# The first stage of a hybrid layer kernel in another order: conditioning and token norms among the filters, float32 filters, loads on three queues

## The chip, the cores and the metric

The kernel runs on one core of a Trainium2 chip. A core has five engines with an instruction stream each: TensorE (PE, matmuls and transposes), VectorE (DVE), ScalarE (ACT), GpSimd (POOL) and SyncE (SP), which here only issues transfers. Sixteen DMA engines move data between HBM and the on-chip memory SBUF; matmuls write to PSUM, which has eight banks. The engines meet through semaphores. The metric is the device time of one execution in microseconds (us); a kernel's time is the median of its runs.

## The reference, cut to what matters

The layer takes 1024 latent tokens, 256 context tokens and two conditioning vectors, in float32. What the change touches stands first:

```python
ada_x = jnp.split(silu(c) @ w_ada[l] + b_ada[l], 6, axis=-1)      # w_ada: 1024 x 6144
ada_c = jnp.split(silu(c_ctx)[None] @ w_ada[l] + b_ada[l], 6, axis=-1)
hc = modulate(rmsnorm(ctx, norm_mix_g[l]), ada_c[0], ada_c[1])    # 256 tokens
hx = modulate(rmsnorm(x, norm_mix_g[l]), ada_x[0], ada_x[1])      # 1024 tokens
h = jnp.sin(z @ w1 + b1); h = jnp.sin(h @ w2 + b2)                # hyena_filters
h = (h @ w3).reshape(L, 2, 2, 512) * jnp.exp(-t * deltas)[:, None, None, :]
Kf = jnp.fft.rfft(k, n=2 * L, axis=0)                             # k: the two sides of h
...
yx, _ = token_mixer(hx, ...)      # w_in projections, Hyena, chunkwise mLSTM, merge
x = x + ada_x[2][:, None, :] * yx
aff = jax.nn.softmax(hx2 @ w_router); gate, idx = lax.top_k(jnp.swapaxes(aff, 1, 2), 128)
ye = (silu(xg @ w1) * (xg @ w3)) @ w2 * gate      # 16 experts, 128 tokens each
return rmsnorm(x + ada_x[5][:, None, :] * scattered_ye, final_norm_g)
```

## The kernel before

Float32 products are made of three matmuls in a rounded format (float32r): each operand is split into a high part (a cast on ACT) and a low part (a subtraction), and `mm3` multiplies high by high, high by low and low by high. A plain float32 matmul needs no split; the profile shows it as two records.

**The first stage** runs to about 165 us. It makes the spectrum of the Hyena filters and the modulated, transposed tokens that the projections multiply.

- `filter_mlp` makes the filter network's hidden rows (`fh`, split into `hl`) and the split last-layer weights (`whh`, `wll`, from the sums `w3sd` that POOL makes). `skip_row` is one small float32 matmul for each order.
- The filters are made in eight units (kind, order, half of the channels). `filter_taps(u)` has 16 matmuls, eight with `whh` on 128 weight rows and eight with `wll` on 64, and four DVE operations that multiply by the decay table `dec` into `fs` (through `fsf`). `filter_dft(u)` multiplies the taps by the DFT table `ft` into four PSUM banks `fe`; `filter_out(u)` combines these on DVE and POOL (`fk_t`, `fk`) and stores them to `K_d`.
- `unit(u)` is `filter_dft(u)`, then `filter_taps(u+2)`, then `filter_out(u)`. Other generators are stepped in between: with `run((a, 1), (some(b, 2), 1))` a step of one stands in the program behind a step of the other.
- `ada_group(0)` is the conditioning: eight slabs `wada` of 1 MB, four matmuls for each into `ada`, four transposes `adaT`. Four slab buffers exist, so slab 4 is loaded when slab 0 has been multiplied. `columns` transposes the small vectors loaded as `R`.
- `norm_tokens` squares and sums token tiles on ACT, makes the reciprocal root (`rq_v`, `rq_r`) on DVE and scales the tiles (`xl`, `xt`) on DVE. `modulated_T` has eight steps for a group of tiles: transposes on PE, scale and shift on ACT or DVE (`hxf`), a split. `gc` makes the context tokens (`hc`), `g0` and `g1` the two halves of the latent tokens (`hx`). The projections that follow start with the matmuls into `pj`, whose weights are `whi` and `wlo`.

All PSUM tiles come from one pool of eight banks; `w2` is a pool of 12 small SBUF tiles. After the filter network the recording layer lets the engines' streams be reordered; the tables of rows further down show the result.

**Later.** The projections and mixers follow, then the router: DVE finds the 128 best tokens of each expert by 16 rounds of MAX8, FIND_INDEX8 and MATCH_REPLACE8. Meanwhile `fill` loads the first expert slabs `er` and splits them into `eh` (ACT) and `el`; with `PAIR` = 4 split slabs made before the experts start, the subtraction of slab 2 is POOL's and those of slabs 0, 1 and 3 are DVE's. The chosen tokens are gathered (`xg`), transposed and modulated by `gather_T` (`xgf`, split into `xgh` and `xgl`), and the experts' matmuls (`pup`, `acc`) start. At the end the final norm takes `rsqrt` of two tiles at a time; POOL multiplies some tiles by the gain `tg`.

Of the kernel before, what the change touches and what calls it, by code (L numbers as in the profile page):

```python
# [103 lines left out]
def layer_kernel(ctx: ExitStack, tc: tile.TileContext, A: dict, out: bass.AP, dbg=None, stop=None):  # L104
# [23 lines left out]
    def w2(shape, dt=F32, name="w"):  # L128
        return wk.tile(shape, dt, name=name, tag="w2", bufs=12)
# [104 lines left out]
    def ada_group(g, wtile, ahead=2):  # L234
# [53 lines left out]
    def filter_loads(alA, alB, alC):  # L288
        zt = alB([33, 1024], name="zt", tag="ss0", bufs=4)
# [11 lines left out]
        R3 = w2([16, 128], name="R3")  # L301
        SY.dma_start(R3[0:8], rows("c", 0, 8))
        SY.dma_start(R3[8:16], rows("c_ctx", 0, 8))
        small.update(R3=R3)
# [9 lines left out]
        def last_layer(o):  # L314
            sd = alB([128, 2, 512], name="w3sd", tag=f"ss{o}", bufs=4)
# [11 lines left out]
    def filter_mlp(alA, alB, loads, tables):  # L327
# [3 lines left out]
        h1 = alB([128, 512], name="fh1", tag="ss0", bufs=4)  # L331
# [10 lines left out]
        for _ in range(4):  # L342
            next(tables)
# [11 lines left out]
        for _ in tables:  # L355
            pass

# [10 lines left out]
        conditions()  # L368

    def filter_tables(al, raw_tile, eng):  # L370
        th, tl = (al([128, len(FT), 128], F32R, name=f"ft{v}") for v in "hl")
        filt["tab"] = th, tl
        raws = []
        for j in range(6):
            raws.append(raw_tile(j))
            SY.dma_start(raws[j], A["ft"][:, 3 * j:3 * j + 3].rearrange("p a m -> p (a m)"))
        yield
        for j in range(6):
            hi, lo = (t[:, 3 * j:3 * j + 3].rearrange("p a m -> p (a m)") for t in (th, tl))
            S.copy(hi, raws[j])  # L380
            eng[j].tensor_tensor(lo, raws[j], hi.bitcast(F32), op=OP.subtract)
            yield

    def filter_taps(u, al):

        kind, o, hf = u
        sets = [[al([128, 4, 256], F32R, name="fs", tag=f"ss{units.index(u) % 2}", bufs=4) for _ in range(2)] for _ in range(2)]
        filt["taps", u] = sets
        hl, whh, wll = filt["hl"], filt["whh"], filt["wll"]
        cs = slice(hf * 256, (hf + 1) * 256)  # L390
        for j2 in range(4):
            p = ps()
            h_ = slice(64 * (j2 // 2), 64 * (j2 // 2) + 64)
            for j in range(2):
                jt = j2 * 2 + j
                pj = p[:, j * 256:(j + 1) * 256]
                T.matmul(pj, hl[:, jt * 128:(jt + 1) * 128], whh[:, o, kind, cs], start=True, stop=False)
                T.matmul(pj, hl[h_, jt * 128:(jt + 1) * 128], wll[h_, o, kind, cs], start=False, stop=True)
            f = w2([128, 2, 256], name="fsf")
            js = slice((j2 % 2) * 2, (j2 % 2) * 2 + 2)  # L400
# [16 lines left out]
    def filter_dft(u):  # L417
# [4 lines left out]
        sets, tabs = filt["taps", u], filt["tab"]  # L422
# [14 lines left out]
    def filter_out(u):  # L437
# [22 lines left out]
        for F, E, a, b, op, rs, rev in ((0, V, bc, bo, OP.add, slice(0, 3, 2), 1), (0, G, bc, bo, OP.subtract, slice(1, 4, 2), 1),  # L460
# [7 lines left out]
            else:  # L468
                res = alC([128, 2, 256], name="fk", bufs=6)
# [43 lines left out]
    alC = phase(sfC, "fC", side="right")  # L513
# [3 lines left out]
    xr = [alxl([128, 1024], name="xr", tag="xl", bufs=4) for _ in range(3)]  # L517
# [1469 lines left out]
```

## Time and profile before

| | before |
|---|---|
| median of 3 runs | 2297.56 us (2296.01 to 2298.42) |
| the profiled execution | 2295.03 us, span 2293.3 us |
| mean granted clock of TensorE | 0.971 |
| PE busy | 2172.0 us (95%), 10609 records |
| DVE busy | 1687.1 us (74%) |
| ACT busy | 1246.8 us (54%) |
| POOL busy | 443.5 us (19%) |
| chain that ended last | PE 48%, DVE 1% of the span, the rest too short or not followed |

The span runs from the first to the last instruction of the profile; the execution's own time is 1.7 us longer. "Busy" counts an engine's instructions and not its waits. The matmul clock has two levels; the profile gives it as a share of the full one. A share of busy time is an average over stages with different limits, so the stage that a change touches has to be looked at by itself.

### The profile page before, as it was taken

To read this page: it belongs to the slowest core of one execution; us is meant where nothing else is said; L and a number is where in the kernel's file an instruction comes from. 1 tells how busy PE (TensorE), PEld (TensorE's weight loads), DVE (VectorE), ACT (ScalarE), POOL (GpSimd) and SP (SyncE) were. 2 spreads that over 40 slices of the span, in tenths; PEclk is the share of its full clock that TensorE was granted. 3 is DMA by queue.
4 is the path that set the end of the run, shared out by engine and by line. 5 is a ranking of instruction groups with operands and counts; after the bars stand their busy time and mean duration, and the time that the engine had idled before them with its cause. 6 is when DMAs were issued, how large, how long until landed. Compare 5 with 4: busy or idle time off the path is not lost. (4 is left out here: it accounts for less than half of the span.)

```text
span 2293.3 us, 28327 instructions
## 1 busy us (share of the span) xinstructions
PE 2172.0 (95%) x10609; PEld 1772.4 (77%) x10609; DVE 1687.1 (74%) x1863; ACT 1246.8 (54%) x1398; POOL 443.5 (19%) x382
## 2 busy tenths in 40 slices
PE   6999999999999999999379999999999999999996
PEld 3679887787778788887268888888888888888884
DVE  5784445664446768553869889898888898888897
ACT  2441342324542223222257777777877777777774
POOL 3563101111124544042200111100111100011001
PEclk9879999999999999999689999999999999999998
DMA  7243335555563333864769999999999999999993
GB/s 264 93 139 95 113 114 176 176 195 190 177 199 114 110 115 124 300 223 147 271 216 386 380 386 382 378 379 393 381 385 384 379 377 396 380 386 383 380 349 141
DMA packets 234793, 605.18 MB, mean 264 GB/s; under 512 B 17722, under 2 KB 89462, under 8 KB 231456
## 3 DMA queue, kind: packets, MB, share of 16 engines
q1 hardware_dynamic: 216752, 551.44, 65.7%
q0 software_dynamic: 12128, 41.43, 5.7%
q10 hardware_dynamic: 5776, 10.50, 1.2%
q8 instruction: 83, 1.36, 0.2%
q14 instruction: 54, 0.44, 0.1%
HBM read 539.34 MB, written 63.98 MB: 263 GB/s over the span
## 5 line engine op out<-in xcount | busy, mean ns | idle before, releaser
L98 DVE TENSOR_TENSOR el<-er,eh 128x2048 fp32r<-128x2048 f32 x383 | 874.4, 2290 | 115.4 <-ACT eh L98 102.5
L98 ACT CAST eh<-er 128x2048 fp32r<-128x2048 f32 x384 | 733.7, 1915 | 236.6 <-PE pup L98 169.1
L98 PE MATMUL pup<-eh,xgh 128*128 128x512 f32 x1024 | 319.7, 393 | 1.6 <-ACT xgh L98 1.6
L98 PE MATMUL pup<-eh,xgl 128*128 128x512 f32 x1024 | 316.7, 390 | 0.0
L98 PE MATMUL ps<-hx,whi 128*128 128x512 f32 x960 | 305.4, 399 | 0.0
L98 PE MATMUL pup<-el,xgh 128*128 128x512 f32 x1024 | 274.4, 390 | 0.0
L98 PEld LDWEIGHTS pup<-eh,xgl 128*128 128x128 f32 x1024 | 192.7, 188 | 40.9 <-DVE xgl L98 0.2
L98 PEld LDWEIGHTS pup<-el,xgh 128*128 128x128 f32 x1024 | 192.6, 188 | 40.4
L98 PEld LDWEIGHTS pup<-eh,xgh 128*128 128x128 f32 x1024 | 190.3, 188 | 40.4 <-ACT xgh L98 2.0
L98 PEld LDWEIGHTS ps<-hx,whi 128*128 128x128 f32 x960 | 178.8, 189 | 40.3 <-ACT nt L98 0.8
L98 POOL DMA_INDIRECT acc_d<-ye,idxc x15 | 50.8, 3390 | 747.5 <-DVE ye L98 747.5
L98 PE MATMUL ps<-hx,wlo 128*128 128x512 f32 x480 | 189.9, 396 | 0.0
L98 PE MATMUL acc<-eh,gh 128*128 128x512 f32 x512 | 161.6, 397 | 0.2 <-ACT gh L98 0.2
L98 PE MATMUL acc<-eh,gl 128*128 128x512 f32 x512 | 160.2, 394 | 0.0
L98 PE MATMUL acc<-el,gh 128*128 128x512 f32 x512 | 139.5, 394 | 0.0
L98 PEld LDWEIGHTS acc<-eh,gl 128*128 128x128 f32 x512 | 96.0, 188 | 22.9 <-DVE gl L98 0.4
L98 PEld LDWEIGHTS acc<-el,gh 128*128 128x128 f32 x512 | 96.2, 188 | 22.4
L98 PEld LDWEIGHTS acc<-eh,gh 128*128 128x128 f32 x512 | 95.0, 188 | 21.6 <-ACT gh L98 0.5
L98 PEld LDWEIGHTS ps<-hx,wlo 128*128 128x128 f32 x480 | 90.5, 188 | 21.2
L98 PE MATMUL pg<-hx,gwh 128*128 128x512 f32 x320 | 103.2, 405 | 3.7 <-ACT gwh L98 3.7
L98 ACT ACTIVATE pb<-ps,colv 128x512 f32<-128x512 f32 (+1 forms) x44 | 29.3, 665 | 129.9 <-PE ps L98 122.2
L98 POOL DMA_INDIRECT xg<-xn_d,idxc x16 | 44.9, 2806 | 260.2 <-PE ps L98 226.1
(374 smaller groups left out, 3393.2 us busy)
## 6 DMA issues: line engine op xcount, KB each, us to landing
er<-in_w_exp_dram SPq DMA_DIRECT2D x384, 1024.0 KB, 7.6
wada<-in_w_ada_dram SPq DMA_DIRECT2D x24, 1024.0 KB, 5.0
wraw<-in_w_in_dram SPq DMA_DIRECT2D x30, 512.0 KB, 4.3
K_d<-fk SPq DMA_DIRECT2D x32, 256.0 KB, 2.2
Kt<-K_d SPq DMA_DIRECT2D x16, 512.0 KB, 5.7
v1c<-v_d SPq DMA_DIRECT2D x20, 256.0 KB, 8.0
gwr<-in_w_in_dram SPq DMA_DIRECT2D x20, 256.0 KB, 6.3
eo_d<-eost POOLq DMA_DIRECT2D x16, 256.0 KB, 7.0
```

Source lines behind the costliest of these rows:

```text
L98: r = op(*a, **k)
```

## The change

- The loads of `c` and `c_ctx` go first on SP. The first four `wada` slabs and the token tiles 0 to 7 are issued by POOL, the DFT tables by ACT.
- The order becomes: token loads, conditioning vectors, filter network, `columns`, all eight steps of `ada_group(0)`, the second `last_layer` and `skip_row`, then taps 0 and 1 and the units. The norms and `gc`, `g0` are stepped from unit 0 on; two steps of `g1` stand in the last `filter_dft`.
- `ft` and `fs` stay in float32: no split of either, and `filter_dft` has 16 float32 matmuls for each unit in place of 48 in float32r.
- `filter_taps` takes four PSUM banks at once and runs its eight `whh` matmuls, then its eight `wll` ones.
- `fill` gives POOL the subtractions of the first four slabs. `gather_T` of the first expert has its second half scaled on DVE in place of ACT.
- The final norm's two steps with constants (`v*inv+eps`, `1.5-0.5*v`) are done by ACT.

```diff
-            SY.dma_start(t, w_ada[len(ts) * 128:(len(ts) + 1) * 128, g * 2048:(g + 1) * 2048])
+            (G if g == 0 and len(ts) < ahead else SY).dma_start(t, w_ada[len(ts) * 128:(len(ts) + 1) * 128, g * 2048:(g + 1) * 2048])
...
+    def filter_tables(al):
+        ft = al([128, len(FT), 128], name="ft")
+        filt["tab"] = ft
         for j in range(6):
+            S.dma_start(ft[:, 3 * j:3 * j + 3], A["ft"][:, 3 * j:3 * j + 3])
...
+        for high in (True, False):
+            for jt in range(8):
+                tap(jt, high)
         for j2 in range(4):
...
-            hi, lo = sets[j2 // 2]
-            S.copy(hi[:, js], f)
-            (V if u == units[0] else G).tensor_tensor(lo[:, js], f, hi[:, js].bitcast(F32), op=OP.subtract)
...
-                    mm3(p[:, h * 256:(h + 1) * 256], [x[:, i] for x in tabs], [x[:, k % 4] for x in sets[k // 4]],
-                        j == 0, j == 1)
+                    T.matmul(p[:, h * 256:(h + 1) * 256], tab[:, i], sets[k // 4][:, k % 4], start=j == 0, stop=j == 1)
...
-            SY.dma_start(toks[i], src)
+            (G if i < 8 else SY).dma_start(toks[i], src)
...
+    load_tokens(0, 1, 2, 3, 4, 5, 6, 7)
+    load_small()
+    conditions()
+    filter_mlp(alA, alB, fl)
     in_order[0] = False
+    columns()
+    for _ in ag0:
+        pass
     filt["last_layer"](1)
     filt["skip_row"](1)
-    load_tokens(0, 1, 2, 3)
-    run((filter_taps(units[1], alB), 1), (some(ag0, 1), 1))
+    run((filter_taps(units[0], alB), 1))
+    run((filter_taps(units[1], alB), 1))
...
+    unit(0, (nt, 1))
+    run((nt, 1))
+    unit(1, (some(gc, 4), 1), (nt1, 1))
+    unit(2, (gc, 1))
...
+    unit(3, (some(g0, 4), 1), (nt1, 1))
+    unit(4, (some(g0, 2), 1), (nt, 1))
+    unit(5, (some(g0, 1), 1))
...
+    unit(6, (g0, 1))
+    run((filter_dft(units[7]), 1), (some(g1, 2), 1))
...
-            (G if i == 2 else V).tensor_tensor(lo, raws[i], hi.bitcast(F32), op=OP.subtract)
+            (G if i < PAIR else V).tensor_tensor(lo, raws[i], hi.bitcast(F32), op=OP.subtract)
...
+                    if on[n]:
+                        S.activation(f[:, k], src, AF.Identity, scale=sc, bias=sh)
+                    else:
+                        V.tensor_scalar(f[:, k], src, sc, sh, op0=OP.mult, op1=OP.add)
...
+        S.activation(v, ss, AF.Identity, scale=inv, bias=cs2[:, 0:1])
...
+        S.activation(v, v, AF.Identity, scale=-0.5, bias=cs2[:, 1:2])
```

On PE, at the start of the program, these rows stood before (`sil` is the activated conditioning vector, `fh` and `fw` the filter network, `whh` and `wll` the taps' weights):

```order
L98 MATMUL ps<-zt,fw_116 64x512 x2
L98 MATMUL ps<-fh_161,fw_120 64x512 x2
L98 MATMUL ps<-fw_127,fh_162 1x512
L98 MATMUL ps<-cst,sil 128x16
L98 MATMUL ps<-whh,hl 128x256
L98 MATMUL ps<-wll,hl 128x256
L98 MATMUL ps<-whh,hl 128x256
L98 MATMUL ps<-wll,hl 128x256
```

Now the same place reads as follows, up to the first DFT:

```order
L98 MATMUL ps<-cst,sil 128x16
L98 MATMUL ps<-zt,fw_119 64x512 x2
L98 MATMUL ps<-fh_187,fw_123 64x512 x2
L98 MATMUL ps<-fw_127,fh_188 1x512
L98 MATMUL ps<-cst,R_171 128x128
L98 MATMUL ps<-cst,R_176 128x44
L98 MATMUL ada<-wada,s_pad 32x512 x32
L98 MATMUL adaT<-cst,ada_sb 128x128 x4
L98 MATMUL ps<-fw_128,fh_188 1x512
L98 MATMUL ps<-whh,hl 128x256 x8
L98 MATMUL ps<-wll,hl 128x256 x8
```

All 32 `ada` matmuls now stand ahead of the first taps, where they used to be spread over units 0 to 3 and the taps of unit 1, and the taps' matmuls stand in two blocks of eight.

On POOL, behind its first small settings, these rows stood before (`w3sd` and `wll` belong to the filters' last layer, `ftl` is the low part of the tables, `fs` the low part of the taps):

```order
L98 MEMSET afp 128x192
L98 ISA
L98 TENSOR_TENSOR w3sd<-fw_127 128x512 x2
L98 TENSOR_TENSOR wll<-w3sd,whh 128x1024
L98 TENSOR_TENSOR ftl<-xr,fth 128x384 x4
L98 TENSOR_TENSOR w3sd<-fw_128 128x512 x2
```

Now POOL's stream begins with twelve transfers; the brackets name the semaphores that a row waits for, and DMASW0 to DMASW3 rise when slabs 0 to 3 have landed:

```order
L98 DMA wada<-in_w_ada_dram 128x2048 x4
L98 DMA xl<-in_ctx_dram 128x1024 x2
L98 DMA xt<-in_x_dram 128x1024 x2
L98 DMA xt<-in_x_dram 128x1024 [waits DMASW0_49]
L98 DMA xt<-in_x_dram 128x1024 [waits DMASW1_49]
L98 DMA xl<-in_x_dram 128x1024 [waits DMASW2_49]
L98 DMA xl<-in_x_dram 128x1024 [waits DMASW3_49]
L98 MEMSET afp 128x192
L98 ISA
L98 TENSOR_TENSOR w3sd<-fw_127 128x512 [waits DMAHW7_49,DMAHW6_49]
```

POOL's first `w3sd` therefore stands behind the landing of the first four slabs.

On DVE, in the router's search for the best tokens, this is the fifth and sixth round before:

```order
L98 MAX vals<-aw 48x8
L98 TENSOR_TENSOR el<-er,eh 128x2048
L98 MATCH_REPLACE aw<-vals,aw 48x512
L98 MAX_INDEX idxu<-vals,aw 48x8
L98 MAX vals<-aw 48x8
L98 TENSOR_TENSOR el<-er,eh 128x2048
L98 MATCH_REPLACE aw<-vals,aw 48x512
L98 MAX_INDEX idxu<-vals,aw 48x8
```

Now the rounds follow one another, and POOL has the four subtractions ahead of its gather of the tokens:

```order
L98 DMA grow_9220<-in_b_ada_dram 128x1024
L98 TENSOR_TENSOR el<-er,eh 128x2048 x4
L98 DMA xg<-xn_d,idxc 128x1024
```

Three `el` rows have left DVE's stream between the router's result and the end of the search; POOL's one became four.

## Rows read from the trace of the kernel before

**Rows 1.** The page's second part: busy tenths of PE in 40 slices of 57 us.

```profile
PE   6999999999999999999379999999999999999996
```

**Rows 2.** Busy time by stretch, with granted clock, DMA share and GB/s.

```profile
core 0: us, PE busy (x) PEld busy (x) DVE busy (x) ACT busy (x) POOL busy (x), PEclk, DMA share, GB/s
...
24.00:165.00 141.00, 132.51 (x643) 94.87 (x643) 98.08 (x170) 57.10 (x102) 67.36 (x52) 0.86 0.43 155
...
60.00:150.00 90.00, 85.83 (x438) 64.81 (x438) 67.31 (x119) 40.20 (x75) 50.98 (x42) 0.80 0.28 94
...
1165.00:2240.00 1075.00, 1075.00 (x4888) 887.25 (x4887) 960.51 (x563) 839.15 (x655) 95.00 (x30) 1.00 1.00 378
```

**Rows 3.** PE's timeline, 24 to 49 us: start, duration, then operation.

```profile
24.70 0.58 PE L98 MATMUL ps<-whh,hl 128*128 128x256 f32 x1
...
32.86 1.86 PE L98 MATMUL ps<-fw,fh 64*1 64x512 f32 x2
...
36.69 1.93 PE L98 MATMUL ada<-wada,s_pad 128*32 128x512 f32 x8
...
48.34 1.05 PE L98 MATMUL ada<-wada,s_pad 128*32 128x512 f32 x2
```

**Rows 4.** Transfers from 0 to 60 us: GB/s in 40 slices of 1.5 us.

```profile
GB/s 0 118 54 6 276 235 216 330 373 240 352 336 385 202 1 257 415 410 431 437 426 421 401 407 410 180 93 382 224 0 0 0 104 377 418 412 407 369 22 0
```

**Rows 5.** PE's timeline: a DFT's end and the taps behind it.

```profile
98.14 0.40 PE L98 MATMUL fe<-fs,fth 128*128 128x256 f32 x2
...
98.50 0.40 PE L98 MATMUL fe<-fs,fth 128*128 128x256 f32 x2
...
99.51 0.38 PE L98 MATMUL ps<-wll,hl 64*128 64x256 f32 x1
99.82 0.39 PE L98 MATMUL ps<-whh,hl 128*128 128x256 f32 x1
...
103.04 0.58 PE L98 MATMUL ps<-whh,hl 128*128 128x256 f32 x1
```

**Rows 6.** PE's timeline, 162 to 179 us: the projections' start and `g1`'s transposes.

```profile
162.41 0.39 PE L98 MATMUL pj<-whi,hch 128*128 128x264 f32 x1 [2.83 <-ACT whi L98]
...
164.99 0.59 PE L98 MATMUL pj<-wlo,hch 128*128 128x264 f32 x1 [0.41 <-DVE wlo L98]
...
177.56 0.39 PE L98 MATMUL pj<-whi,hx 128*128 128x264 f32 x1 [1.08 <-DVE hx L98]
177.78 1.03 PE L98 MATMUL ps<-cst,xl 128*128 128x128 f32 x8
```

**Rows 7.** DVE's timeline in the router's search, 1119 to 1127 us.

```profile
1119.70 0.67 DVE L98 MAX8 vals<-aw 48x8 f32<-48x512 f32 x1
...
1121.75 0.67 DVE L98 MAX8 vals<-aw 48x8 f32<-48x512 f32 x1
1122.34 2.26 DVE L98 TENSOR_TENSOR el<-er,eh 128x2048 fp32r<-128x2048 f32 x1
...
1125.86 0.67 DVE L98 MAX8 vals<-aw 48x8 f32<-48x512 f32 x1
```

**Rows 8.** POOL's timeline beside that search.

```profile
1116.65 4.52 POOL L98 TENSOR_TENSOR el<-er,eh 128x2048 fp32r<-128x2048 f32 x1 [0.89 <-ACT eh L98]
1155.33 1.03 POOL L98 DMA_INDIRECT xg<-xn_d,idxc  x1 [34.17 <-DVE idxl L98]
```

**Rows 9.** The experts' start: PE's first matmul, ACT's work ahead of it.

```profile
1163.46 1.22 PE L98 MATMUL pup<-eh,xgh 128*128 128x512 f32 x2 [1.65 <-ACT xgh L98]
...
1161.04 1.86 ACT L98 ACTIVATE xgf<-ps,AB 128x128 f32<-128x128 f32 x5 [42.68 <-issue]
```

**Rows 10.** The tail's timelines: DVE's constant steps and POOL's product.

```profile
2270.97 0.16 DVE L98 TENSOR_SCALAR rq_v<-rq_v 128x2 f32<-128x2 f32 x1
...
2278.12 2.26 DVE L98 TENSOR_SCALAR rq_v<-rq_v 128x2 f32<-128x2 f32 x1
...
2278.02 2.34 POOL L98 TENSOR_TENSOR xf<-xf,tg 128x1024 f32<-128x1024 f32 x1 [1.54 <-ACT xf L98]
```

More of the change, by code (lines that the diff above doesn't have):

```diff
@@ L288, in filter_loads @@
     def filter_loads(alA, alB, alC):
-        zt = alB([33, 1024], name="zt", tag="ss0", bufs=4)
+        R3 = w2([16, 128], name="R3")
+        SY.dma_start(R3[0:8], rows("c", 0, 8))
+        SY.dma_start(R3[8:16], rows("c_ctx", 0, 8))
+        small.update(R3=R3)
+        zt = alB([33, 1024], name="zt", tag="ss0", bufs=3)
         SY.dma_start(zt, A["zT"])
@@ L325, in filter_loads, with filter_mlp @@
         return zt, w1, bb, w2_, w3
-    def filter_mlp(alA, alB, loads, tables):
+    def filter_mlp(alA, alB, loads):
         zt, w1, bb, w2_, w3 = loads
-        h1 = alB([128, 512], name="fh1", tag="ss0", bufs=4)
+        h1 = alB([128, 512], name="fh1", tag="ss0", bufs=3)
         h2 = alB([128, 512], name="fh2", tag="ss1", bufs=4)
@@ L341, in filter_mlp @@
         p = ps()
-        for _ in range(4):
-            next(tables)
         for n in range(2):
@@ L367, in filter_mlp @@
         skip_row(0)
[L368 to L373, printed above, removed]
-        for j in range(6):
[L375 to L382, printed above, removed]
+    def filter_tables(al):
+        ft = al([128, len(FT), 128], name="ft")
+        filt["tab"] = ft
+        for j in range(6):
+            S.dma_start(ft[:, 3 * j:3 * j + 3], A["ft"][:, 3 * j:3 * j + 3])
     def filter_taps(u, al):
         kind, o, hf = u
-        sets = [[al([128, 4, 256], F32R, name="fs", tag=f"ss{units.index(u) % 2}", bufs=4) for _ in range(2)] for _ in range(2)]
+        sets = [al([128, 4, 256], name="fs", tag=f"ss{units.index(u) % 2}", bufs=3 + units.index(u) % 2) for _ in range(2)]
         filt["taps", u] = sets
@@ L390, in filter_taps, with tap @@
         cs = slice(hf * 256, (hf + 1) * 256)
-        for j2 in range(4):
[L392 to L400, printed above, removed]
+        pt = [ps() for _ in range(4)]
+        def tap(jt, high):
+            pj = pt[jt // 2][:, (jt % 2) * 256:(jt % 2 + 1) * 256]
+            h_ = slice(0, 128) if high else slice(64 * (jt // 4), 64 * (jt // 4) + 64)
+            T.matmul(pj, hl[h_, jt * 128:(jt + 1) * 128], (whh if high else wll)[h_, o, kind, cs], start=high and jt % 2 == 0, stop=not high and jt % 2 == 1)
+        for high in (True, False):
+            for jt in range(8):
+                tap(jt, high)
+        for j2 in range(4):
+            p = pt[j2]
+            f = sets[j2 // 2][:, (j2 % 2) * 2:(j2 % 2) * 2 + 2]
             V.scalar_tensor_tensor(f, p.rearrange("p (j c) -> p j c", j=2), -1.0 if kind and j2 > 1 else 1.0,
@@ L516, in layer_kernel @@
     fl = filter_loads(alA, alB, alC)
-    xr = [alxl([128, 1024], name="xr", tag="xl", bufs=4) for _ in range(3)]
-    ft0 = filter_tables(alB, lambda j: xr[j // 2][:, (j % 2) * 512:(j % 2) * 512 + 384], [G, G, G, G, V, V])
-    next(ft0)
+    filter_tables(alB)
     dec = alA([128, 8, 512], name="dec")
@@ L560, in unit @@
         run((filter_out(units[u]), 1), *more)
-    unit(0, (some(ag0, 1), 1))
-    columns()
-    load_tokens(4, 5, 6, 7)
-    nt = norm_tokens(0, 1, 2, 3)
-    unit(1, (some(ag0, 2), 1), (some(nt, 2), 1))
-    unit(2, (some(ag0, 2), 1), (nt, 1))
-    nt = norm_tokens(4, 5, 6, 7)
-    unit(3, (ag0, 1), (nt, 1))
     sada.close()
-    sfC.close()
     AB = cp.tile([128, 2, 2, 8], F32, name="AB")
@@ L619, in layer_kernel @@
     g1 = hx_gen(1)
-    unit(6, (some(g0, 2), 1))
-    run((filter_dft(units[7]), 1))
+    unit(6, (g0, 1))
+    run((filter_dft(units[7]), 1), (some(g1, 2), 1))
     sfB.close()
@@ L1888, in layer_kernel, with rsqrt_s @@
     warm = late([128, 1], F32, name="warm")
+    cs2 = late([128, 2], F32, name="cs2")
+    V.memset(cs2[:, 0:1], EPS)
+    V.memset(cs2[:, 1:2], 1.5)
+    def rsqrt_s(ss, n, inv):
+        v, r = sm([128, n], name="rq_v"), sm([128, n], name="rq_r")
+        S.activation(r, ss, AF.Sqrt, scale=inv, bias=cs2[:, 0:1])
+        S.activation(v, ss, AF.Identity, scale=inv, bias=cs2[:, 0:1])
+        V.reciprocal(r, r)
+        V.tensor_tensor(v, v, r, op=OP.mult)
+        V.tensor_tensor(v, v, r, op=OP.mult)
+        S.activation(v, v, AF.Identity, scale=-0.5, bias=cs2[:, 1:2])
+        V.tensor_tensor(r, r, v, op=OP.mult)
+        return r
     tg = spare([128, 2, 1024], name="tg")
```

30 lines of the change are left out of this document (10 added, 20 removed).

## The prediction, made before the changed kernel was run

> **What bounds the kernel now.** I read the busy slices first [rows 1]: PE is full nearly everywhere, and the places where it is not are the start, the dip near 1110 to 1165 us and the end. The change edits just these three, so each is costed by the engine that is late there. Between 1165 and 2240 us PE is busy for all of 1075 us [rows 2], so whatever the experts' start gains is still there at the end; I take the same of the mixer stages between. For the first stage I then read the windows: from 24 to 165 us PE is busy for 132.5 of 141 us and DVE for 98.1 [rows 2]. PE is the bound there, and it doesn't run at its full level: the mean granted clock from 60 to 150 us is 0.80 [rows 2]. The stage's end is the first matmul into `pj` at 162.41 and the first with `wlo` at 164.99 [rows 6].
>
> **First stage: PE's own work.** A tap matmul follows the last one after 0.31 us at the full level (99.51 to 99.82), while three DFT matmuls of the same 256 columns take 0.36, or 0.12 each (98.14 to 98.50) [rows 5]. The taps alternate between 128 and 64 weight rows. The extra 0.19 can belong to the change of rows, or the pair's 0.38 to the 64-row matmul itself. In the first case a unit's 16 taps now cost 16 x 0.12 and two changes, 2.3 us, in the second 5.0 as before; over eight units the ends are 22 us apart. A 64-row float32 matmul of 512 columns (`skip_row`) took 1.86 us at the lower level [rows 3], which is 0.93 at the full one; four transposes of 128 columns, float32 too and on 128 rows, took 1.03 there [rows 6]. So 64 rows alone cost nothing extra. I take 2.3. The Trainium skill, TensorEngine Tiling (Array Packing), section Tiling Modes, says that a change of the tiling mode, other than of the tile, drains the engine; by that rule the grouping is worth its 22 us at the full level, and by a price of the 64-row matmul itself it would be worth nothing.
>
> A unit's DFT was 48 matmuls of 0.12, 5.8 us. Now it is 16 in float32. Their price from the same `skip_row`: 1.86 us for 512 columns at the lower level is 0.46 for 256 at the full one; from the transposes, eight records (four transposes of 128 columns) in 1.03 [rows 6], 0.4 to 0.5 for 256. I take 0.43: 6.9 us for a unit, 1.1 more than before. Beside this, `gc` and `g0` with 16 steps and two steps of `g1` are 3.2 + 6.4 + 1.6 us (0.4 for the two transposes of a `gc` step, 0.8 for the four of the others). From the first tap to the first `pj` PE then has 8 x 2.3 + 8 x 6.9 + 11.2 = 84.8 us of work at the full level.
>
> **First stage: the late start.** Taps began at 24.70 [rows 3]. They now stand behind all eight `ada` steps, and these behind the slabs. By the tiles' shapes 16.9 MB move first (eight slabs 8.4, eight token tiles 4.2, `dec` 2.1, tables 1.2, last-layer weights 1.0), and some 0.3 of small loads. The slices move 400 to 437 GB/s when large tiles are queued and 330 to 385 with `dec` and smaller ones [rows 4]. The first 13 MB take 32 us at 410; the last four slabs wait for buffers, so they start when `ada` does, and 4.2 MB take 10 us more. POOL's queue waits for slabs to land ahead of its first `w3sd`, and PE's `skip_row` and `ada` stand behind what follows from it, so `ada` doesn't start before about 32 us either way. An `ada` step is 1.93 us at the lower level and 1.05 at the full one [rows 3]; the slabs, not PE, set the pace. With the last step, the copy, `adaT` and `skip_row` behind the landing at 44 to 47 I put the first tap at 52 us (48 to 60). The Trainium skill, DMA: Bandwidth & Descriptors, section Issuing engines are not separate DMA queues, says that loads started from several engines share the same 16 engines and only save issue time; by that rule three queues bring no bandwidth and the sum of bytes above holds, whereas if a second queue doubled the rate the start would be near 35. The slices at 437 from SP alone [rows 4] agree with the rule.
>
> **First stage: what PE waits for.** DVE loses only the few splits that it had and what moves ahead of the taps, and gains two steps of `g1`: of its 98.1 us I keep 92 (85 to 98). So DVE, not much shorter than before, is now as long as PE's 84.8, and where DVE has all eight PSUM banks (the taps take four at once) PE waits. I add 8 us for the difference and 4 for ends of units and for `whi` (2.83 [rows 6]). PE comes from `ada` steps with gaps, and before the change it was at the lower level there (0.58 per tap, 1.93 per step [rows 3], whatever the clock column says); two units of taps and half a DFT at that level are 8 us more. Sum: 52 + 84.8 + 12 + 8 = 157 for the first `pj`, against 162.41: -6. The two `g1` steps taken out of the projections (0.8 each) and the waits there for `hx` (one of 1.08 [rows 6]; with a first half ready earlier it goes) are -3. First stage: -9, from -24 (first tap at 48, no cold units, 8 us of waits) to +5 (first tap at 60, full low-level units). ACT's casts and POOL's subtractions of `fs` (POOL was busy for 67 of 141 us [rows 2]) I cost at nothing: the taps are made two units ahead of their DFT. If that cover is gone, taking them away gains up to 2 us a unit for units 0 and 1.
>
> **The experts' start.** A round of the search takes 2.05 us (1119.70 to 1121.75) and one with an `el` 4.11 (1121.75 to 1125.86) [rows 7]. Three go: -6.2. POOL's four at 4.52 are 18 us from 1116, so done near 1134, ahead of its gather at 1155 [rows 8]; that idle stretch is the cover, and without it the gather would be later by what sticks out. POOL's subtraction ran beside rounds of unchanged length. ACT had five `xgf` of 0.35 ahead of the first `xgh`, now four; PE's first `pup` waited for `xgh` [rows 9]: -0.3. Sum -6.5 (-4.5 to -7).
>
> **The tail.** A constant step takes 0.16 us on DVE, but 2.26 when POOL's product of 2.34 starts just before [rows 10]; the chain of waits has three of these, 6.3 us too long together. On ACT they aren't held, but ACT has squares and a scaling of 1.1 us each ahead of them. I take half: -3.5 (0 to -6).
>
> **Sum.** -9 - 6.5 - 3.5 = -19 on the profiled execution's 2295.0: 2276. The runs' median lies 2.5 above that execution: 2278.5.
>
> **The rivals.** (a) The clock decides, and the result is slower. Half as many but four times as long matmuls make a low level dear: the DFTs alone then cost 13.8 us a unit. PE's 84.8 us need 106 at the mean of 0.80 that 60 to 150 us had, about what I forecast with its waits; they need 128 at 0.66, the forecast's 105 and 23 more, and then the 19 are gone and about 2302 is reached. Against it: in the trace the level fell while alternating taps ran (0.39 a matmul at 99.82, 0.58 at 103.04 [rows 5]), and these go; float32 matmuls keep PE denser. For it: PE's new waits for DVE. 8 in 100. (b) The start is later than 60: `R` and the last-layer weights stand behind the large tiles in three queues, and the first tap comes at 65. Then the first stage gives +4 and the sum is -6: 2291.5. 14 in 100. (c) The later edits give nothing, since POOL's four subtractions and ACT's chain are late themselves: 2288.5. 10 in 100. (d) PE is dense and at the full level from the first unit: -24 - 6.5 - 4 gives 2263. 16 in 100. My forecast has 52.
>
> **The numbers.** 0.2%, 4.6 us, is about what a measurement of this kernel can tell from no change. Faster by more than that (below 2293) are the forecast, (c), (d) and two thirds of (b): 0.88. (a) is slower in five cases of eight, 0.05; the rest, 0.07, lies within. The range of 2265 to 2291 leaves out (a), some of (b) and the far end of (d). The likeliest's own is 2271 to 2285.
>
> **What would show it.** First tap at 52 and 16 tap matmuls in 2.3 us at the full level; 16 float32 matmuls of 0.43; PE waiting for DVE at the DFTs' starts; first `pj` at 157. Rounds of 2.05 throughout the search and the first `pup` 6.5 us nearer to the search's start. No `rq_v` above 0.3 us at the end. Wrong would be a granted clock below 0.7 between 52 and 157, a first tap past 60, taps still at 5 us a unit, or PE waiting for slabs after 1165.

## The result and the profile after

The changed kernel takes 2279.01 us (median of 4, 2277.28 to 2282.55) against 2297.99 (2296.01 to 2302.77) for the kernel before, measured together with it: a ratio of 0.9921, 95% interval 0.9907 to 0.9934. The prediction was 2278.5, within 2265 to 2291. The time came out as forecast, but not by the steps of the forecast: the start was 11 us later and PE's stretch behind it some 15 us shorter than forecast, a wait for weights was twice its size, and the tail's term gave nothing. That these errors cancel is luck.

The profiled execution took 2278.72 us, its span 2277.0. Four landmarks place the difference to the span of 2293.3 before: the first tap, the first `pj`, the first MAX8 of the search and the experts' first `pup`. The rows of before for them are [rows 3, 6, 9]; the first MAX8 is this row of DVE's timeline, before and after:

```profile
1113.55 0.69 DVE L98 MAX8 vals<-ps 48x8 f32<-48x512 f32 x1 [1.14 <-PE ps L98]
```

```profile
1103.54 0.69 DVE L98 MAX8 vals<-ps 48x8 f32<-48x512 f32 x1 [1.14 <-PE ps L98]
```

| us | before | after | after minus before |
|---|---|---|---|
| first tap | 24.70 | 63.27 | +38.6 |
| first `pj` | 162.41 | 157.90 | -4.5 |
| first MAX8 of the search | 1113.55 | 1103.54 | -10.0 |
| first MAX8 to first `pup` | 49.91 | 43.51 | -6.4 |
| first `pup` to the end | 1129.84 | 1129.95 | +0.1 |

The page's second part after, PE's busy tenths, and the windows (columns as in [rows 2]):

```profile
PE   2989999999999999999289999999999999999996
```

```profile
24.00:63.00 39.00, 17.45 (x78) 2.93 (x74) 11.48 (x17) 5.85 (x9) 10.89 (x8) 0.91 0.70 260
63.00:150.00 87.00, 84.11 (x441) 70.72 (x440) 78.29 (x152) 36.13 (x65) 34.38 (x26) 0.96 0.26 88
60.00:150.00 90.00, 86.40 (x454) 71.22 (x446) 78.86 (x157) 38.02 (x68) 34.38 (x26) 0.96 0.25 85
1147.00:2220.00 1073.00, 1072.95 (x4871) 885.38 (x4872) 957.43 (x563) 836.35 (x653) 94.06 (x29) 1.00 1.00 377
```

PE's first slice fell from 6 to 2 tenths [rows 1]: between 24 and 63 us it works for 17.45 of 39 us, where it had taps before. From then on it is dense, and at 0.96 of its full level between 60 and 150 us where it had 0.80 [rows 2]. The experts are as full as they were.

PE's timeline after, which answers to [rows 3], and its last DFT and first projections, which answer to [rows 6]:

```profile
34.62 1.86 PE L98 MATMUL ps<-fw,fh 64*1 64x512 f32 x2 [9.18 <-ACT fh L98]
41.99 0.45 PE L98 MATMUL ps<-cst,R 128*128 128x128 f32 x1 [5.50 <-DMA R<-in_hy_conv_dram]
...
43.14 5.55 PE L98 MATMUL ada<-wada,s_pad 128*32 128x512 f32 x32
50.25 1.06 PE L98 MATMUL ada<-wada,s_pad 128*32 128x512 f32 x8 [1.56 <-DMA wada<-in_w_ada_dram]
...
59.30 1.73 PE L98 MATMUL ada<-wada,s_pad 128*32 128x512 f32 x8 [0.55 <-DMA wada<-in_w_ada_dram]
...
63.27 1.22 PE L98 MATMUL ps<-whh,hl 128*128 128x256 f32 x8
64.42 0.75 PE L98 MATMUL ps<-wll,hl 64*128 64x256 f32 x8
65.10 1.21 PE L98 MATMUL ps<-whh,hl 128*128 128x256 f32 x8
...
66.92 7.17 PE L98 MATMUL fe<-fs,ft 128*128 128x256 f32 x32
...
145.91 3.62 PE L98 MATMUL fe<-fs,ft 128*128 128x256 f32 x16
157.90 0.59 PE L98 MATMUL pj<-whi,hch 128*128 128x264 f32 x1 [8.37 <-ACT whi L98]
...
159.42 0.57 PE L98 MATMUL pj<-wlo,hch 128*128 128x264 f32 x1
```

Four slabs are multiplied in one go at 43.14: they had long landed (POOL's waits for them end by 23.86), and PE waited for `R`. A unit's 16 taps take 65.10 - 63.27 = 1.83 us, its DFT 6.8 (66.92 to 73.74, where the next tap starts). The last DFT ends at 149.5; then PE stands 8.37 us for `whi`. The queue of SP and ACT's cast show that wait's other end:

```profile
96.52 55.80 SPq L400 DMA_DIRECT2D K_d<-fk  x23
152.43 1.06 SPq L630 DMA_DIRECT2D wraw<-in_w_in_dram  x2
```

```profile
156.78 1.07 ACT L98 CAST whi<-wraw 128x1056 fp32r<-128x1056 f32 x1 [6.47 <-DMA wraw<-in_w_in_dram]
```

The first projection weights stand on SP behind 23 stores of filters, each of which waits for its `fk`; they land 4.3 us after their issue (152.43 to 156.78).

The search and the experts' start after (DVE, POOL and PE; [rows 7 to 9] before):

```profile
1105.62 0.67 DVE L98 MAX8 vals<-aw 48x8 f32<-48x512 f32 x1
...
1107.66 0.67 DVE L98 MAX8 vals<-aw 48x8 f32<-48x512 f32 x1
...
1109.71 0.67 DVE L98 MAX8 vals<-aw 48x8 f32<-48x512 f32 x1
```

```profile
1105.78 17.95 POOL L98 TENSOR_TENSOR el<-er,eh 128x2048 fp32r<-128x2048 f32 x4
1139.12 1.03 POOL L98 DMA_INDIRECT xg<-xn_d,idxc  x1 [15.38 <-issue]
```

```profile
1147.05 1.22 PE L98 MATMUL pup<-eh,xgh 128*128 128x512 f32 x2 [1.49 <-ACT xgh L98]
```

All rounds take 2.04 to 2.08 us, and POOL is done at 1123.7, 15 us ahead of its gather. The tail after, which answers to [rows 10]:

```profile
2256.69 2.31 DVE L98 TENSOR_TENSOR rq_v<-rq_v,rq_r 128x2 f32<-128x2 f32 x1
...
2262.67 2.40 DVE L98 TENSOR_TENSOR rq_v<-rq_v,rq_r 128x2 f32<-128x2 f32 x2
...
2268.07 2.19 DVE L98 TENSOR_TENSOR rq_v<-rq_v,rq_r 128x2 f32<-128x2 f32 x2
```

```profile
2256.38 2.61 POOL L98 TENSOR_TENSOR xf<-xf,tg 128x1024 f32<-128x1024 f32 x1 [30.34 <-ACT xf L98]
2262.52 2.34 POOL L98 TENSOR_TENSOR xf<-xf,tg 128x1024 f32<-128x1024 f32 x1 [3.53 <-ACT xf L98]
2267.72 2.34 POOL L98 TENSOR_TENSOR xf<-xf,tg 128x1024 f32<-128x1024 f32 x1 [2.86 <-issue]
```

The steps with constants have left DVE, as the change says. The next small step there, a product of `rq_v` and `rq_r`, is now the one that lies beside POOL's product, and takes its length.

### The profile page after: what moved, and what is told of

It reads as the page before. It is cut to its first block, busy times and chain, and to the rows that moved or that the text cites. A ratio compares the mean times of both kernels' runs of the same rounds, so it can differ in the third digit from the quotient of the medians.

```text
span 2277.0 us, 27985 instructions
## 1 busy us (share of the span) xinstructions
PE 2139.1 (94%) x10481; PEld 1752.9 (77%) x10481; DVE 1657.0 (73%) x1852; ACT 1226.9 (54%) x1364; POOL 422.9 (19%) x365
## 5 line engine op out<-in xcount | busy, mean ns | idle before, releaser
L98 PEld LDWEIGHTS acc<-eh,gh 128*128 128x128 f32 x512 | 95.0, 188 | 21.5 <-ACT gh L98 0.5
```

Of the source, the lines that this page charges most:

```text
L98: r = op(*a, **k)
```

## The experiments

Times are medians. The kernel before had 2297.96, 2295.18, 2294.86 and 2294.90 us in the four sets of runs, so kernels of different sets are compared by their difference to it. Landmarks are read from one profile of each kernel and carry an uncertainty of some 6 us up to the first MAX8: `e2_before_late` below has the first stage of before unchanged, and its first MAX8 stands at 1120.20 in place of 1113.55.

**Is it the grouping?** `e1_taps_alt` is the changed kernel with the taps alternating again:

```diff
-        for high in (True, False):
-            for jt in range(8):
+        for jt in range(8):
+            for high in (True, False):
                 tap(jt, high)
```

> The changed kernel with each unit's taps alternating between 128 and 64 weight rows again; the four banks at once and all else stay. If the extra 0.19 us belongs to the change of rows, a unit's taps take 5.0 us again in place of 1.9 at the full level: 8 x 3.1 = 25 us of PE work come back and some 15 to 25 us of time, more where the clock falls to the lower level while they run (the granted clock between the first tap and the first projection goes from above 0.9 to about 0.8). If it belongs to the 64-row matmul itself, nothing changes (the changed kernel's own blocks already speak against this). If DVE sets the pace of the units, less than 10 us come back.

Measured: 2312.05 (2309.03 to 2316.57), ratio to before 1.0066 (1.0047 to 1.0085). PE's timeline and window:

```profile
64.37 0.58 PE L98 MATMUL ps<-whh,hl 128*128 128x256 f32 x1
64.88 0.58 PE L98 MATMUL ps<-wll,hl 64*128 64x256 f32 x1
65.39 0.58 PE L98 MATMUL ps<-whh,hl 128*128 128x256 f32 x1
```

```profile
63.00:182.00 119.00, 117.89 (x418) 85.41 (x417) 78.16 (x150) 33.74 (x61) 29.25 (x24) 0.81 0.19 62
```

A tap follows the last after 0.51 us here, and the granted clock falls from 0.96 to 0.81. From first tap to the end of the last DFT PE needs 122.6 us (64.37 to 192.82 less the wait of 5.86) where the grouped kernel needs 86.2. Of these 36 us, 128 taps by 0.31 less 0.114 (the full level's prices, [rows 5] and 1.83 / 16) are 25; the rest is the lower level, in taps (32 of them in a row at 0.51 from 64.37) and in the DFTs behind them. Without the grouping the change would have made the kernel 14 us slower.

`e7_before_grouped` is the other side: the kernel before with one edit, taps in groups of four (two PSUM banks) for each pair of steps.

```diff
+                for high in (True, False):
+                    for j in range(4):
...
+                        if high:
+                            T.matmul(pj, hl[:, jt * 128:(jt + 1) * 128], whh[:, o, kind, cs], start=j % 2 == 0, stop=False)
+                        else:
+                            T.matmul(pj, hl[h_, jt * 128:(jt + 1) * 128], wll[h_, o, kind, cs], start=False, stop=j % 2 == 1)
```

> The kernel before with one edit: the taps of four tiles are made together, four matmuls on 128 weight rows and then four on 64, in place of an alternation. Its DFT in three passes, its early first tap (24.7 us) and its loads stay. Theory: the alternation costs PE both the drain at each change and the level of its clock; grouped, a unit's taps take some 2.5 us in place of 5 and more, the granted clock from 60 to 150 us rises from 0.80 to 0.93 or more, DVE's 98 us become the bound, and the first pj comes at 130 to 142 in place of 162.4: 2298 - 25 = 2273 (2266 to 2280), which is below the changed kernel. Rival: DVE and the filters' loads set the pace of the stage, and the first pj comes at 152 or later: 2288 or more.

Measured: 2272.96 (2270.49 to 2275.26), ratio 0.9903 (0.9880 to 0.9927), with the first `pj` at 139.63. This one edit does as much as the whole change (22 us below before against 19). The level did not rise as far as the theory said: the granted clock from 60 to 150 us is 0.87, not 0.93, and PE now waits for DVE five times between 60 and 110 us, up to 3.25 us at a time and 9.7 in all.

**Where do the 11 us at the start come from?** `e6_sp_queue` is the changed kernel with POOL's transfers (slabs and tokens) issued by SP at the same places of the program; `e4_small_first` keeps the queues and loads `R` ahead of the last-layer weights and the tokens behind the slabs; `e5_small_first_sp` does both.

```diff
-            (G if g == 0 and len(ts) < ahead else SY).dma_start(t, w_ada[len(ts) * 128:(len(ts) + 1) * 128, g * 2048:(g + 1) * 2048])
+            SY.dma_start(t, w_ada[len(ts) * 128:(len(ts) + 1) * 128, g * 2048:(g + 1) * 2048])
...
-            (G if i < 8 else SY).dma_start(toks[i], src)
+            SY.dma_start(toks[i], src)
```

```diff
+        load_small()
         w3 = [alB([128, 2, 512], name="fw3", tag="ss1", bufs=4) for _ in range(2)]
...
-    load_tokens(0, 1, 2, 3, 4, 5, 6, 7)
-    load_small()
     conditions()
...
     for _ in ag0:
         pass
+    load_tokens(0, 1, 2, 3, 4, 5, 6, 7)
```

> The changed kernel with slabs 0 to 3 and tokens 0 to 7 issued by SP, in the same order of the program; only the queue of these twelve loads differs. Theory: the large loads that POOL starts at 1.4 us hold up the small ones that the filter network waits for (fb landed at 18.9 us, before the change at 5.6). Then fb lands near 6 us and the second fh is made near 20 in place of 34; but the small vectors R now stand behind twelve large loads on one queue, and the first tap stays within 55 to 65 us: the time moves by less than 5 us either way. If three queues bring bandwidth, the first tap comes more than 5 us later than 63.3 and the time is 5 to 15 us longer.

> As the kernel with the small vectors first and the tokens behind the slabs, but with slabs 0 to 3 and the tokens issued by POOL as in the changed kernel. If large loads on another queue hold up small ones, fb lands near 15 to 19 us, the second fh comes after 27 and the first tap 4 to 8 us later than with SP alone: 50 to 55, and the time falls by 8 to 13 us against the changed kernel. If the queues make no difference, both kernels agree within 2 us.

> The changed kernel with all first-stage loads but the tables on SP, and in another order: the small vectors R ahead of the last-layer weights and the decay table, the tokens behind the eight slabs. Theory: the late first tap (63.3 us) is one of order, since the last R was issued at 41.4 behind the decay table and slabs 4 to 7 wait for it. Then the ada steps start near 25 us, slabs 4 to 7 follow at once and the first tap comes at 44 to 50: the time falls by 12 to 17 us. Rival, bytes: 17 MB at 400 GB/s and a start of 8 us put the first tap at 50 whatever the order, but the tokens' 4 MB now come behind it, so it would be 40 to 45. Rival, DVE or the projections' weights set the end of the stage: the first tap comes earlier and the first projection doesn't; the time stays within 4 us.

| | changed kernel | e6 | e4 | e5 |
|---|---|---|---|---|
| filter biases `fb` used by DVE | 18.88 | 8.30 | 17.84 | 8.51 |
| first `skip_row` (filter network done) | 34.62 | 24.46 | 32.73 | 23.87 |
| first transpose of `R` | 41.99 | 40.71 | 34.53 | 25.66 |
| first `ada` | 43.14 | 41.61 | 35.19 | 26.34 |
| first tap | 63.27 | 62.78 | 56.47 | 46.50 |
| first `pj` | 157.90 | 157.13 | 152.11 | 141.35 |
| time | 2279.01 | 2276.86 | 2273.22 | 2263.90 |
| ratio to before, interval | 0.9921 (0.9907, 0.9934) | 0.9912 (0.9895, 0.9928) | 0.9888 (0.9866, 0.9909) | 0.9845 (0.9829, 0.9861) |

Two chains of small loads end late, side by side, and the later one decides: PE's `skip_row` stands behind the filter network, which needs `fb`, and `ada` stands behind `skip_row` and the transposes of `R`. DVE's timeline of the changed kernel shows the first, SP's queue the second, and the transfers of its first 60 us (GB/s in 40 slices of 1.5 us, as [rows 4]) what comes of both:

```profile
18.88 0.16 DVE L98 COPY fb<-fb 64x2 f32<-64x2 f32 x1 [6.34 <-DMA fb<-in_hy_f_b_dram]
```

```profile
34.54 0.30 SPq L210 DMA_DIRECT2D R<-in_ml_conv_dram  x1
41.40 0.25 SPq L211 DMA_DIRECT2D R<-in_ml_norm_g_dram  x1
45.14 3.95 SPq L240 DMA_DIRECT2D wada<-in_w_ada_dram  x4
```

```profile
GB/s 0 155 282 298 316 382 403 351 393 411 370 282 285 267 291 275 295 313 401 400 395 410 393 411 399 377 150 11 1 0 82 246 410 284 377 415 410 431 137 5
```

The two `fb` loads of 0.2 KB are issued at 3.5 and 5.8 us, among slabs of 1 MB that POOL started at 1.35, and are there at 18.9; with the slabs behind them on SP they are there at 8.3 (e6) and 8.5 (e5). By PE's waits `R`'s first tile is complete at 41.9, though its last piece was issued at 25.39; the second tile's last piece is issued at 41.40; both stand behind the large loads. The sixteen DMA engines then run dry (11, 1, 0 GB/s near 42 us): slabs 4 to 7 wait for buffers that `ada` frees only after `R`. Putting only one chain right (e6: `fb`; e4: `R`) gains 0.5 and 6.8 us of the first tap; both together gain 16.8. From the first `ada` to the first tap all four kernels need 20 to 21 us. One thing is not separated: e4 and e5 also move the tokens' 4.2 MB behind the slabs, and `R` ahead with the tokens in their place was not run.

In e5 the first tap is 16.8 us earlier and the time 15 us lower. So the start of the changed kernel was on the path.

**The wait for `whi`.** `e8_all` is e5 with the first projection weights issued by ACT, and with the final norm as in `e3_tail_dve` below:

```diff
-                SY.dma_start(raw[:, :, o:o + m], w_in[kh * 512:(kh + 1) * 512, c0:c0 + m].rearrange("(k p) n -> p k n", p=128))
+                (S if turn[0] < 2 else SY).dma_start(raw[:, :, o:o + m], w_in[kh * 512:(kh + 1) * 512, c0:c0 + m].rearrange("(k p) n -> p k n", p=128))
```

> The changed kernel with three things: all its first loads on SP in the order of their use (small loads, last-layer weights and R, decay, slabs, then tokens), the first projection weights issued by ACT in place of SP, and the final norm without POOL's products. Theory: the first two bring the first tap to 46 to 47 us and the wait for whi from 8.6 to some 6, the last 2 to 4 us at the end: 2264 - 5 = 2259 (2254 to 2263). Rival: the first projection weights wait for their tile's memory and not for SP, and the end stays as it was: 2264.

Measured: 2257.22 (2248.63 to 2259.28), ratio 0.9839 (0.9816 to 0.9862). The first tap stays at 46.52. ACT's queue and PE's first `pj`:

```profile
129.14 1.00 ACTq L98 DMA_DIRECT2D wraw<-in_w_in_dram  x2
```

```profile
134.56 0.46 PE L98 MATMUL pj<-whi,hch 128*128 128x264 f32 x1 [4.80 <-ACT whi L98]
```

The wait is 4.80 in place of e5's 8.59, and most of it is the 4.3 us from issue to landing (129.14 to 133.44): the load waited for its place in SP's queue, not for memory alone. In time this edit and the tail's together give some 4 us: 38.0 below before against e5's 34.1, which their intervals don't separate.

**The later edits.** `e2_before_late` is the kernel before with only `fill`, `gather_T` and the root on ACT from the change; the diff is that part of the change.

> The kernel before with only the edits of its late stages: three of the four subtractions of the experts' first weights moved to POOL, every second cast of the gathered tokens on DVE, and the constant steps of the final norm's root on ACT. Theory: the search's rounds all take 2.05 us and the first pup comes 6.4 us nearer to the first MAX8, while the tail stays as long as it was, since POOL's product then holds DVE's next step with two inputs: 2298 - 6 = 2292 (2290 to 2294). Rival: the tail does give its 3.5 us on this kernel and the changed kernel lost them elsewhere: 2288.5. Second rival: the first-stage gain and this one hang together, and alone this gives nothing: 2298.

Measured: 2287.77 (2284.24 to 2298.46), ratio 0.9971 (0.9956 to 0.9986). In its trace the first MAX8 to the first `pup` takes 43.93 us, 6.0 less than before, and the first `pup` to the end 1129.57, as before. The times alone (7.4 us less, 3 to 10 by the interval) would allow the rival's 9.5 us; the landmarks do not.

`e3_tail_dve` is the changed kernel with the products of all eight tiles on DVE:

```diff
-                if tt in (0, 2, 4):
-                    S.activation(xt[:, ns], src, AF.Identity, scale=r)
-                else:
+                if True:
...
-            if tt in (0, 2, 4):
-                G.tensor_tensor(xt, xt, tg[:, 1], op=OP.mult)
-                later.append(tt)
-            else:
-                store(tt)
+            store(tt)
```

> The changed kernel with the final norm's products of tiles 0, 2 and 4 taken from ACT and POOL and made by DVE like the other five, one step each. Theory: POOL's product is what stretches DVE's steps rq_v to 2.2 to 2.4 us; with no such product on POOL they take some 0.1 us each, three stretches of 2 us go, and DVE has three products more (1.1 us each): the stretch from the last matmuls to the end is 2 to 4 us shorter, 2279 - 3 = 2276. Rival 1: the steps are long of themselves or for another reason: they stay above 2 us and the time is 2279 or, with DVE's three more products, 2282. Rival 2: DVE and the stores set the end in any case: rq_v falls to 0.1 us and the end stays within 1 us of what it was.

Measured: 2275.05 (2270.92 to 2279.96), ratio 0.9909 (0.9890 to 0.9927). The same steps of DVE near the end, with nothing on POOL beside them:

```profile
2260.36 0.15 DVE L98 TENSOR_TENSOR rq_v<-rq_v,rq_r 128x2 f32<-128x2 f32 x1
...
2266.07 0.16 DVE L98 TENSOR_TENSOR rq_v<-rq_v,rq_r 128x2 f32<-128x2 f32 x1
...
2271.16 0.36 DVE L98 TENSOR_TENSOR rq_v<-rq_v,rq_r 128x2 f32<-128x2 f32 x2
```

The stretch from the first `rq_r` reciprocal to the end is 21.5 us (2256.72 to 2278.2) in place of 24.5 (2252.52 to 2277.0). Three held steps go, some 6 us, and three products of 1.28 come to DVE. The medians alone would not show it: 20.1 us below before against the changed kernel's 19.0.

**Float32, the rest, and what the new start costs.** `e12_grouped_f32` adds the single float32 pass to e7: `ft` is loaded into its tile, `fs` is written directly, and the DFT has one matmul where `mm3` had three. `e10_grouped_late` is e7 with the late edits of e2 and the norm of e3 instead.

> The kernel before with the taps grouped in fours and, in addition, the DFT in one float32 pass in place of three passes of split halves (tables loaded straight into their tile, no casts on ACT, no subtractions on POOL); the early first tap stays. Theory: a unit's DFT takes PE 6.8 us in place of 5.8, 8 us in all, of which PE's waits for DVE (some 12 us with three passes) take most: the first pj within 4 us of the 139.6 that the grouping alone has, 2273 (2269 to 2277); float32 by itself gives nothing here. Rival 1: float32 keeps PE's granted clock up (0.96 in place of 0.87 between 60 and 150 us) and takes casts off the path: first pj at 132 or earlier, 2265 or less. Rival 2: PE is the bound and its 8 us come on top: 2281.

> The kernel before with the taps grouped in fours (first pj at 139.6 us, 2273 alone), the late edits (the subtractions on POOL, the casts on DVE: -6.4) and the final norm without POOL's products (-3.3); the first stage's order, loads and three-pass DFT are those of before. Theory: the three places lie one after another on PE's path and add up: 2273 - 6.4 - 3.3 = 2263 (2260 to 2267), 16 below the changed kernel, so that the rebuilt start of the first stage loses by itself. Rival: the earlier end of the first stage collides with something between, and the sum isn't reached: 2268 or more.

e10 measured 2264.05 (2263.36 to 2266.57), ratio 0.9870 (0.9854 to 0.9887): the three places add up, as expected. e12 measured 2265.53 (2262.30 to 2267.04), ratio 0.9870 (0.9853 to 0.9886), and there the theory fell: float32 gives 7 us more than the grouping alone. `e13_grouped_f32_late` below and e10 differ by the same edit, and there too it gives 7 us (38.1 below before against 30.8). The window from 60 to 130 us in e7 and in e12:

```profile
60.00:130.00 70.00, 58.75 (x374) 50.38 (x375) 61.77 (x106) 36.43 (x68) 46.20 (x37) 0.88 0.28 95
```

```profile
60.00:130.00 70.00, 66.90 (x343) 52.33 (x342) 61.16 (x123) 27.62 (x52) 26.05 (x21) 0.98 0.32 111
```

Float32 gives PE more work, takes 9 us of ACT and 20 of POOL, and has PE busy for 8 us more of the 70 at 0.98 in place of 0.88. In e7 PE waited in this window for DVE steps (`fk_t`, `hxf`, `adac`); in e12 two such waits are left, 1.43 and 1.67. The first `pj` and the first MAX8 of e7 and of e12:

```profile
139.63 0.59 PE L98 MATMUL pj<-whi,hch 128*128 128x264 f32 x1 [1.87 <-ACT whi L98]
...
1091.62 0.69 DVE L98 MAX8 vals<-ps 48x8 f32<-48x512 f32 x1 [1.14 <-PE ps L98]
```

```profile
138.37 0.59 PE L98 MATMUL pj<-whi,hch 128*128 128x264 f32 x1 [6.72 <-ACT whi L98]
...
1085.54 0.69 DVE L98 MAX8 vals<-ps 48x8 f32<-48x512 f32 x1 [1.15 <-PE ps L98]
```

The first `pj` did come within 4 us of e7's, as the theory had it: PE is done 6 us earlier and then stands 6.72 us for `whi` in place of 1.87. But the gain is not lost there, since the first MAX8 is 6.1 us earlier. Behind the first `pj` PE waits three times more in e7 (1.42 for `fk_t`, 0.47 and 1.09 for `hx`, up to 157 us) and not in e12. How much the shorter way from tap to DFT gives and how much the level was not taken apart.

`e13_grouped_f32_late` is e12 with the late edits and the norm of e3, so that against e3 only the first stage differs: the order of conditioning, norms and taps, the queues, and taps in fours from two PSUM banks in place of eights from four. `e14_grouped_f32_late_act` adds the weights issued by ACT, the edit of e8.

> The kernel before with grouped taps, the DFT in one float32 pass, the late edits and the final norm without POOL's products; nothing else of the changed kernel: taps still begin at 24 us, token norms and slabs stay where they were, loads on SP. Theory: 2265.5 - 6.4 - 3.3 = 2256 (2252 to 2260), as much as the changed kernel has after its loads are put in the order of their use (2257): the rebuilt start of the first stage is worth nothing that the early taps don't have. Rival: DVE, busy for 61 of 70 us in that stage, gets in the way, or the gain of float32 was that of one run: 2263.

> The kernel of the other run of this call with the first projection weights issued by ACT in place of SP. Theory: these loads stand on SP behind the filters' stores (11 of them issued from 109 to 132 us), and PE's wait of 6.7 us for whi falls by 3 to 4, as it fell from 8.6 to 4.8 when the changed kernel's were moved: 3 to 4 us below the other run. Rival: they wait for memory that the filters free, and the wait stays: the two agree within 1 us.

e13 measured 2256.76 (2254.59 to 2261.22), ratio 0.9831 (0.9806 to 0.9855); e14 2251.12 (2247.55 to 2255.05), ratio 0.9805 (0.9780 to 0.9830). PE between 24 and 63 us in e13, to be read beside the changed kernel's first window above, and e14's first projections:

```profile
24.00:63.00 39.00, 39.00 (x168) 26.27 (x168) 18.97 (x33) 6.80 (x13) 5.28 (x3) 1.00 0.88 337
```

```profile
127.60 0.39 PE L98 MATMUL pj<-whi,hch 128*128 128x264 f32 x1
...
130.94 0.39 PE L98 MATMUL pj<-wlo,hch 128*128 128x264 f32 x1 [0.51 <-DVE wlo L98]
```

With the start of before, PE has taps and DFTs to do for all 39 us in which the slabs land; in the changed kernel it stands for more than 21 of them. e13 is 38.1 us below before and e3 20.1: the new start costs 18 us, give or take 7 by the two intervals. Putting its loads in the order of their use gives 15 of these back (e5). With that and `whi` issued by ACT the new start is at 38.0 below before (e8), against 43.8 with the start of before and the same edit for `whi` (e14); the intervals of these two overlap.

In e14, which differs from e13 by the issuing engine alone, the wait for `whi` is gone (6.29 us in e13), and it gains 5.6, more than the 3 to 4 expected. Not all of this need be the edit: PE is ahead by 2.1 us at 93 us already (92.94 against 95.04 for the same transposes), long before the loads. It is the fastest kernel of the study: 43.8 us below before, where the changed kernel is 19.0 below.

So the change's 19 us are a sum of a gain and a loss. By the medians against before: grouping -22, float32 -7, the late edits -7, the new start +18, which is -18. By the traces' landmarks, the first MAX8 is at 1113.55 before, 1091.62 with the grouping, 1085.54 with float32 and 1103.54 in the changed kernel: -21.9, -6.1, +18.0, each uncertain by the 6 us above; the experts' start gives the other -6.4, the tail nothing.

## Why the prediction came out, point by point

**Taps: right.** The forecast was 2.3 us a unit and 22 us of worth for the grouping, from the gap of 0.31 to 0.12 [rows 5]. Measured: 1.83 us a unit, 22 us alone (e7), 33 in the changed kernel (e1), where the lower level comes on top. That e7's number is the forecast's is partly luck: it has groups of four, its level rose from 0.80 to 0.87, and PE's waits for DVE took some of that back. The Trainium skill, TensorEngine Tiling (Array Packing), section Tiling Modes, says that a change of mode drains the engine; e1 and e7 agree with that rule, and a price of the 64-row matmul itself is out (eight of them follow one another in 0.68 us, 64.42 to 65.10). The grouping also parts the two matmuls of a pair, which add into the same piece of PSUM; that this was the price is unlikely, since `mm3`'s matmuls in the DFT before add into one piece one behind the other too, at 0.12 each [rows 5].

**DFT: the price right, the worth of float32 not.** A unit's DFT took 6.8 us against 6.9. But the forecast put the casts and subtractions that float32 saves at nothing, so float32 stood in its sum as 8 x 1.1 = 8.8 us of loss. In the order of before it gives 7 us of gain (e12 against e7, e13 against e10); in the changed kernel's own order it was not run alone.

**The first tap: mis-sized, 52 forecast and 63.3 measured.** The sum of bytes was sound, and from the first `ada` to the first tap 20 us went by, as forecast. What failed is the sentence that `ada` starts near 32 us: it was taken from the landing of the slabs and POOL's `w3sd`, and `ada` started at 43.14, because small loads (`fb`, `R`) came behind or among large ones. That was rival (b), given 14 in 100; its mechanism happened for `R`, and `fb` it did not name. e5 bears it out: with the small loads ahead and the tokens behind, `ada` starts at 26.34. The forecast's 1.05 for an `ada` step at the full level came from a row with two of a step's eight records [rows 3]; the changed kernel has all eight in 1.06 (50.25).

The rule on issuing engines that the forecast weighed (the Trainium skill, DMA: Bandwidth & Descriptors, section Issuing engines are not separate DMA queues) also says that transfers of all queues interleave. e6 agrees that the other queues bring no time (2276.86 against 2279.01). What the forecast left out is the interleaving's effect on small loads, `fb` at 18.88 in place of 8.30.

**PE's waits for DVE (8 of the 12) and the low level of the first units (8): all but absent.** From first tap to the end of the last DFT PE took 86.2 us against a forecast work of 84.8; by the measured prices the work was 80.2 (8 x 1.83 + 8 x 6.8 + 11.2). DVE was busy for 78 of the 87 us there, so it was nearly as long as PE, but PE waited three times, 2.4 us together; and the level was full from the first tap. That is rival (d)'s mechanism, given 16 in 100, with (b)'s start. The low level is small where it occurs: e3's first stage is the same program, its first taps ran at it (a unit in 3.17 us, 65.54 to 68.71), and the stretch took 88.3 us (65.54 to 153.86).

**The wait for `whi`: mis-sized.** The forecast had 4 us for this and for ends of units; it was 8.37, since SP issues the weights behind the filters' stores. e8 and e14 settle the cause.

Together: +11 at the start, about -15 in the units, +4 or more at `whi`, and the first `pj` came at 157.9 where 157 was forecast. The first stage's -9 was measured as -10.0: -4.5 at the first `pj`, where the forecast rounded 5.4 to 6, and -5.5 behind it, where it had 3. One profile's 6 us are larger than these differences.

**The experts' start: right.** -6.4 for a forecast of -6.5, for the reasons given: all rounds at 2.04 to 2.08 us, POOL done ahead of its gather. e2 shows it alone, with -6.0.

**The tail: wrong, 0 for -3.5.** The step that failed is that the constant steps were what POOL's product holds. In the changed kernel, with the constants on ACT, it held the DVE step that came next, the product of `rq_v` and `rq_r`. e3 took POOL's product away, and the stretch to the end was 3 us shorter.

**The rivals (a) and (c)** did not occur: the granted clock was 0.96, and the experts' edits gave their part. The forecast's own chances for a time below 2293 add up to 0.87, where it wrote 0.88.

## What to carry to other kernels

A block of matmuls that alternates between 128 and 64 weight rows is worth sorting before anything else is moved: here one loop order alone gave 22 us, the whole change 19. Before work that needs loads is moved to the front, look for what PE can do while they land, and put the few small loads that gate it ahead of the large ones, whichever queue these are on. A step moved off an engine gains nothing if the next step there is held by the same neighbour; take the neighbour away.

## What the runs showed of the hardware

- Alternating taps cost 0.31 us each at the full level of TensorE's clock [rows 5] and 0.51 at the lower one (e1); sorted into eights they cost 0.114 (1.83 for 16). The granted clock is low in the stretch with alternating taps, 0.81 in e1, and near the top with sorted taps and float32 DFTs, 0.96.
- Eight `wll` matmuls, four on each half of the weight rows, take 1.16 us at the lower level (e3, 67.55 to 68.71), as long as four on one half (e7, 26.02 to 27.17, 1.15 us); eight `whh` on 128 rows take 2.01 (e3, 65.54 to 67.55). So matmuls on the two halves seem to run side by side, which would make groups of eight better than groups of four. No run was made for this alone.
- Two loads of 0.2 KB issued at 3.5 and 5.8 us arrived by 18.9 among 1 MB slabs of another queue (changed kernel) and by 8.3 with the slabs behind them on the same queue (e6).
- POOL's product of 2.34 us on two SBUF tensors stretches a DVE step of 128x2 elements from 0.15 to 2.3 us, with a constant [rows 10] or with two inputs in SBUF (`rq_v`, after). The Trainium skill, SBUF — State Buffer, section Who interferes with whom, says that a DVE instruction with two SBUF inputs, or in a 2-port mode, and a GpSimd one that reads SBUF exclude each other; e3 agrees for the two-input step, 0.15 us once POOL is idle.
- In the start of the changed kernel DVE's steps of the sine take 4.38 us for two beside POOL's `w3sd` and `wll`, from 29.07 us, and 1.42 at 20.88 without them.
